# The hybrid layer's third up product at 256 columns, z in groups of 272/384/384 at one distance, weight tiles of one size, and splits on VectorE

## The chip, the core and the metric

The kernel runs on one core of a Trainium2 chip. The time is the device time of one execution in microseconds; the figure that counts is the median over several executions. Before the change it is 1257.54 us (three runs, 1257.53 to 1258.32).

A core has a matrix engine (TensorE, PE in the profile, with its weight loads shown apart as PEld), three engines for elementwise work (VectorE or DVE, ScalarE or ACT, GpSimd or POOL) and an engine that issues most of the DMA transfers (SyncE or SP). The engines run on their own and wait for each other by semaphores. Operands lie in SBUF, 128 partitions wide; matmul results are collected in PSUM.

## What is computed

One layer of a hybrid decoder in float32, on 1024 tokens with 16 meta tokens in front (1040 rows) and width 1024:

```python
h = layer_norm(concat([meta, x]), in_ln_g, in_ln_b)
z = h @ w_in + b_in
q, k, v, c_in, gates = split(z)            # 512, 128, 128, 1024, 2048
a = swa_sink_attention(q, k, v, sinks)     # window 128, 8 heads, 2 kv heads
c = c_val * sigmoid(c_gate)                # halves of c_in
c = silu(layer_norm(causal_dwconv(c, conv_dw, conv_dw_b)))   # 31 taps
mixed = sigmoid(g_attn) * (a @ w_attn_proj) + sigmoid(g_conv) * (c @ w_conv_proj)
h = layer_norm(alpha * h + mixed @ w_out)
up = causal_dwconv(h @ ffn_w_up)           # 2 x 2816 columns, 3 taps
u, g = split(up)
h = layer_norm(alpha * h + (gelu(g) * u) @ ffn_w_down)
return h[:, 16:]
```

## The kernel before

Every matrix product is done in the fp32r type, with both operands split into a high and a low part: for each 128 rows of the contraction there are three matmuls, high by high (L301), high by low (L305) and low by high (L306). The weights are the stationary operand, 128 x 128 at a time, and the activations (transposed, so that tokens run along the free axis) are the moving one.

In order of time the stages are: the opening with the first LayerNorm, the transposes and the first z tiles (0 to 60 us); z tiles with the conv's chunks (60 to 165); attention, with further z tiles as filler between its matmuls (165 to 350); the rest of the gates' z tiles (350 to 416); the two projections and their merging with the gates, by eight output blocks m (416 to 515); the output product with its LayerNorm (515 to 640); the up stage (to 1037); the down stage and the last LayerNorm (to the end).

z: a z tile is 128 columns of w_in, that is, 128 rows of the transposed z, over all tokens. `z_tile` (L316) loads and splits its weights with `weights` (L281) and runs three groups of tokens, 24 matmuls each (8 pieces of the contraction, three matmuls). The groups of the eight conv tiles are ZG: 400, 384 and 256 columns; those of the three q tiles and the sixteen gate tiles are TG, the same without the first 14 tokens: 386, 384 and 256. k, v and the first q tile run in the opening, in the groups HG (272, 384, 384), with matmuls at L514 and L517. The normalized input's high and low parts, the moving operand, lie in the wide tiles RHO (first four pieces of the contraction) and RHC (last four). `h0` (L255) gives their place: piece k, part hl starts at (2k + hl) x 1040 floats, which is 65 times 64 bytes.

Weights: `wraw_p` holds two raw tiles. `wsp_p` holds two pairs of tiles `whi` and `wlo`. A `wlo` tile is 64 columns wider than a `whi` tile; z uses it from column 16 on (`shift=16`), the projections from column 0. The up stage takes the same tiles for the ring of split weights (`wsplit`, L1318), and the last LayerNorm for its rows (`ln_rows`). Counted in units of 64 bytes from the start of a partition, the two `whi` tiles lie at 191 and 255, the two `wlo` tiles at 319 and 387. The raw weights are cast to the high part on ScalarE (L273); the low part is raw minus high (L276), on VectorE for the first 23 tiles that are loaded and on GpSimd for the 15 after them: gates 9 to 15 and the eight blocks of the projections.

Attention's tiles (keys `kx`, values `v`, queries `qt`, scores `s`, probabilities `ph` and `pl`) lie behind the pool `cp` on the right side of SBUF and start 32 bytes off a multiple of 64. Scores are matmuls of 272 columns (L833, L834), sums over values 512 columns (L868 to L870).

The conv on 31 taps runs on VectorE (L669) into four accumulators; `csum` adds them for the conv's LayerNorm, two adds on GpSimd (L886, L887) and one on VectorE (L888).

The up stage uses a Strassen form with seven block products in place of eight, in 22 chunks. A product has two halves of the token columns (`sub` 0 and 1, 258 and 256 columns wide) with 12 matmuls each (L1503). `columns` gives the first column: the first two columns of the first half are left out in two of the seven products, BT3 and B22, which are then 256 wide. `B_AT` says where the right operand of each product lies; that of BT1 in the first half is in the tile RX, at column 16.

The order of work on each engine is set when the program is built, by priorities (`cur_priority`, `rank`) and by extra edges (`after`). `ahead` (L743) is a matmul of gate tile 0, in its second group; the first matmuls of attention are placed behind it.

Of the kernel before, what the change touches and what calls it, by code (L numbers as in the profile page):

```python
# [29 lines left out]
P = 128  # L30
D = 1024
# [17 lines left out]
ALPHA = 2.0 ** 0.25  # L49
NEG = -1e30  # L50


ZG = [(0, 400), (400, 784), (784, 1040)]

HG = [(0, 272), (272, 656), (656, 1040)]
UG = [(0, 258), (258, 642), (642, 1026)]
# [45 lines left out]
def tile_hybrid_layer(  # L102
# [150 lines left out]


    def h0(k, hl, a, b):  # L255
        o = ((k % 4) * 2 + hl) * T
        return (RHO if k < 4 else RHC)[:, o + a:o + b]


    tc.cur_priority = RK_QKV  # L260

    def wsp(name, tag):
        return wsp_p.tile([P, D + (64 if tag == "wlo" else 0)], R, name=name, tag=tag)

    def pair_of(hi, lo, shift=0, shape=None):
        hi, lo = wsp(hi, "whi"), wsp(lo, "wlo")[:, shift:shift + D]
        return [t.rearrange("p (k c) -> p k c", k=KC) for t in (hi, lo)] if shape else [hi, lo]

    def wraw(shape):
        return wraw_p.tile(shape, F, name="wr", tag="wr")  # L270
# [7 lines left out]
    fills = [0]  # L278
    last_fill, last_split = [], []

    def weights(shape, fill, shift=16):  # L281
        fills[0] += 1
        n = fills[0]
        own = n == 3
        raw = sp.tile(shape, F, name="wr3") if own else wraw(shape)
        with rank({1: 13, 2: 18, 3: 17, 4: 23}.get(n, RK_SPLIT)):
            last_fill.append(fill(raw))
        hi, lo = (sp.tile(shape, R, name=t + "3") for t in ("whi", "wlo")) if own else pair_of("whi", "wlo", shift, shape)
        if n <= 3:
            return hi, lo, raw  # L290
        with rank(RK_SPLIT):
            last_split.append(split(raw, hi, lo, n <= 23))
        return hi, lo

    chunks_done = []
# [25 lines left out]
    def in_cols(m):  # L321
        return lambda raw: load(raw, w_z[m])

    TG = [(a + U0 if i == 0 else a, b) for i, (a, b) in enumerate(ZG)]

    st_next = [0]

# [294 lines left out]

    att = ExitStack()
    cp = att.enter_context(tc.tile_pool(name="cin", bufs=2, side="right", reuse_waits="tile"))
    ap = att.enter_context(tc.tile_pool(name="att", bufs=1, side="right", reuse_waits="tile"))

    Kx = [ap.tile([P, NB, 144], R, name=f"kx{g}") for g in range(NKV)]
# [18 lines left out]
    def conv_chunk(c):  # L646
        sig = {}

        def g_evac(g, a, b, ps):
            sig[g] = stage(b - a)  # L650

            nc.scalar.activation(sig[g], ps, AF.Tanh, bias=bcol(10 + c), scale=0.5)
            nc.scalar.activation(sig[g], sig[g], AF.Identity, bias=half_, scale=0.5)

        z_tile(in_cols(10 + c), ZG, g_evac, wt_c1[0] if c == 1 else None)
        cin = cp.tile([P, 16 + T], F, name="cin", tag="cin")
        nc.vector.memset(cin[:, 0:16], 0.0)

        def v_evac2(g, a, b, ps):
            nc.vector.scalar_tensor_tensor(cin[:, 16 + a:16 + b], ps, bcol(6 + c), sig[g], OP.add, OP.mult)  # L660

        z_tile(in_cols(6 + c), ZG, v_evac2, wt_c1[1] if c == 1 else None)
        with rank(RK_CONV + c * 100):
            for j in range(TAPS):
                wc = cdw[:, j * CH + c:j * CH + c + 1]
                if j == 0:
                    nc.vector.tensor_scalar(acc[c], cin[:, j:j + U], wc, cdwb(c), OP.mult, OP.add)
                else:
                    nc.vector.scalar_tensor_tensor(acc[c], cin[:, j:j + U], wc, acc[c], OP.mult, OP.add)  # L669
# [70 lines left out]
    tc.cur_priority = RK_Z - 500  # L740
    first_chunk = len(chunks_done)
    gate_tile(0)
    ahead = chunks_done[first_chunk + KC + 5]  # L743

    tc.cur_priority = RK_ATT

# [130 lines left out]
    for o in order:  # L877
        if isinstance(o, str):
            conv_chunk(int(o[1]))
        else:  # L880
            gate_tile(o)
        if o == "c3":

            csum = cp.tile([P, 16 + T], F, name="csum", tag="cin")[:, :U]
            with rank(RK_EVAC):
                nc.gpsimd.tensor_tensor(csum, acc[0], acc[1], OP.add)  # L886
                nc.gpsimd.tensor_tensor(csum, csum, acc[2], OP.add)  # L887
                nc.vector.tensor_tensor(csum, csum, acc[3], OP.add)  # L888

    def mean_mms(ps, w, hi, lo):  # L890
# [164 lines left out]
    def prep_wo(k, raw=None, behind=None):  # L1055
        if k < 4:
            hi, lo = OA[:, k * 2048:k * 2048 + 1024], OA[:, k * 2048 + 1024:k * 2048 + 2048]
        elif k < 6:
            hi, lo = ((RX, RW)[k - 4][:, x:x + 1024] for x in (0, 1024))
        else:  # L1060
            hi, lo = pair_of("whi", "wlo")
        if raw is None:
            raw = wraw([P, D])
            load(raw, w_out_v[k])
# [17 lines left out]
    tc.cur_priority = RK_PROJ  # L1082
    early = []
    for m in range(KC):
        hi, lo = weights([P, KC, P], lambda raw: load(raw, w_ab[m]), 0)

        def branch(i, g, tag, bufs):
            a, b = PG[g]
# [56 lines left out]
    def quadrant(sub, kk, h):  # L1145
# [1 line left out]
        return FA[:, h1_at(sub, i):h1_at(sub, i + 4)]  # L1147


    B_AT = [[(RHC, 6224), (RHO, 4112), (OA, 16), (RX, 16), (OA, 2096), (OA, 6224), (OA, 4144)],  # L1150
            [(OC, 48), (OC, 2096), (OC, 4144), (OC, 6192), (RHC, 2096), (RHC, 48), (RHC, 4144)]]
    B11, B21, BT2, BT1, BT3, BT4, B22 = range(7)

    def columns(sub, q):

        a, b = SUB[sub]
        return (2 if q in (BT3, B22) else a) if sub == 0 else a, b

    def bsum(sub, q, hl):
        a, b = columns(sub, q)  # L1160
# [152 lines left out]
    def wsplit(src):  # L1313
# [1 line left out]
        ring_next[0] += 1  # L1315
        i %= len(RING)
        if RING[i] is None:
            RING[i] = wsp("ws", ("whi", "wlo")[i % 2])[:, 0:D]  # L1318
        t = RING[i]
        hi, lo = t[:, 0:512], t[:, 512:1024]  # L1320
        nc.scalar.copy(hi, src)  # L1321
# [339 lines left out]
    extra = []  # L1661

    def ln_rows(names):
        return [wsp_p.tile([P, D + (64 if t == "wlo" else 0)], F, name=n, tag=t)[:, 0:D]
                for n, t in zip(names, ("whi", "wlo"))]

    gains = ln_rows(("g1", "b1"))
    g1, b1 = gains
# [127 lines left out]
```

## Time and profile before

| | |
|---|---|
| median of three runs | 1257.54 us |
| profiled execution, its time | 1257.53 us |
| profiled execution, span of the trace | 1255.4 us |
| TensorE busy | 1244.7 us (99% of the span) |
| VectorE busy | 1086.2 us (87%) |
| ScalarE busy | 586.4 us (47%) |
| GpSimd busy | 54.0 us (4%) |
| DMA | 212.10 MB, mean 169 GB/s |

The span is the time from the first to the last record of the trace; the time of the execution has some 2 us around it. A matmul's busy time is longer than its share of the engine, since matmuls overlap in the pipeline: what one costs is the time from its start to the start of the next, and a window that begins at the first matmul of a group and ends at the first of the next holds just that. The chain that ended last is followed back from the last instruction to whatever released it; with 97% on PE, it is a list of matmuls.

### The profile page before, as it was taken

To read this page: it belongs to the slowest core of one execution; us is meant where nothing else is said; L and a number is where in the kernel's file an instruction comes from. 1 tells how busy PE (TensorE), PEld (TensorE's weight loads), DVE (VectorE), ACT (ScalarE), POOL (GpSimd) and SP (SyncE) were. 2 spreads that over 40 slices of the span, in tenths; PEclk is the share of its full clock that TensorE was granted. 3 is DMA by queue.
4 is the path that set the end of the run, shared out by engine and by line. 5 is a ranking of instruction groups with operands and counts; after the bars stand their busy time and mean duration, and the time that the engine had idled before them with its cause. 6 is when DMAs were issued, how large, how long until landed. Compare 5 with 4: busy or idle time off the path is not lost.

```text
span 1255.4 us, 21714 instructions
## 1 busy us (share of the span) xinstructions
PE 1244.7 (99%) x8546; PEld 1178.1 (94%) x8546; DVE 1086.2 (87%) x1859; ACT 586.4 (47%) x1057; POOL 54.0 (4%) x28
## 2 busy tenths in 40 slices
PE   9999999999999999999999999999999999999997
PEld 8999999999999999788899999999999998888886
DVE  7899989999989587548899999999999986995697
ACT  7522244545474223235565555554555554544330
POOL 0000000010112132000000000000000000000000
PEclk9999999999999999999999999999999999999999
DMA  7294733332246565212145555563464569988722
GB/s 279 72 306 108 193 96 97 106 92 84 68 142 177 155 172 140 85 68 101 68 135 192 193 204 192 185 212 115 162 228 166 203 213 319 389 322 300 251 85 84
DMA packets 96152, 212.10 MB, mean 169 GB/s; under 512 B 10787, under 2 KB 35939, under 8 KB 95922
## 3 DMA queue, kind: packets, MB, share of 16 engines
q1 hardware_dynamic: 84282, 199.64, 47.8%
q10 hardware_dynamic: 11768, 11.08, 2.7%
q8 instruction: 67, 1.10, 0.4%
q14 instruction: 35, 0.29, 0.1%
HBM read 150.29 MB, written 62.70 MB: 170 GB/s over the span
## 4 chain that ended last, share of the span: by engine, by line
PE 97%; DVE 1%; ACT 1%; DMA 0%; issue 0%; SPq 0%; DVEq 0%
PE px L1503 15%; PE py L1503 9%; PE ps_x L1641 9%; PE ps_z L305 8%; PE ps_z L301 8%; PE ps_z L306 8%; PE ps_z L1641 7%; PE pz L1503 5%; PE pw L1503 5%; PE ps_p L301 2%; PE ps_p L306 2%; PE ps_p L305 2%; PE ps_w L306 2%; PE ps_w L301 2%; PE ps_w L305 2%; PE ps_z L517 2%
## 5 line engine op out<-in xcount | busy, mean ns | idle before, releaser
L669 DVE SCALAR_TENSOR_TENSOR FA<-cin,cols,FA 128x1026 f32<-128x1026 f32 x120 | 155.2, 1305 | 0.2
L301 PE MATMUL ps_z<-RHO,whi 128*128 128x384 f32 (+2 forms) x324 | 104.6, 323 | 0.0
L305 PE MATMUL ps_z<-RHC,whi 128*128 128x384 f32 (+2 forms) x324 | 104.6, 323 | 0.0
L305 PE MATMUL ps_z<-RHO,whi 128*128 128x384 f32 (+2 forms) x324 | 104.0, 321 | 0.0
L306 PE MATMUL ps_z<-RHC,wlo 128*128 128x384 f32 (+2 forms) x324 | 103.8, 320 | 0.0
L301 PE MATMUL ps_z<-RHC,whi 128*128 128x384 f32 (+2 forms) x324 | 103.7, 320 | 0.0
L306 PE MATMUL ps_z<-RHO,wlo 128*128 128x384 f32 (+2 forms) x324 | 103.4, 319 | 0.0
L1322 DVE TENSOR_TENSOR RHO<-wr,RHO 128x512 fp32r<-128x512 f32 x94 | 63.9, 689 | 5.4 <-ACT RHO L1321 5.4
L1321 ACT CAST RHO<-wr 128x512 fp32r<-128x512 f32 x94 | 56.8, 620 | 23.0 <-DVE wr L1339 12.0
L273 ACT CAST whi<-wr 128x1024 fp32r<-128x1024 f32 x37 | 38.9, 1051 | 53.8 <-PE ps_z L305 32.3
L301 PEld LDWEIGHTS ps_z<-RHO,whi 128*128 128x128 f32 x324 | 60.9, 188 | 0.5 <-issue 0.3
L305 PEld LDWEIGHTS ps_z<-RHC,whi 128*128 128x128 f32 x324 | 60.9, 188 | 0.4
L306 PEld LDWEIGHTS ps_z<-RHC,wlo 128*128 128x128 f32 x324 | 60.9, 188 | 0.2
L301 PEld LDWEIGHTS ps_z<-RHC,whi 128*128 128x128 f32 x324 | 60.9, 188 | 0.2
L306 PEld LDWEIGHTS ps_z<-RHO,wlo 128*128 128x128 f32 x324 | 60.9, 188 | 0.1
L305 PEld LDWEIGHTS ps_z<-RHO,whi 128*128 128x128 f32 x324 | 60.9, 188 | 0.1
L1339 DVE TENSOR_TENSOR wr<-wr 128x512 f32<-128x512 f32 x88 | 60.8, 691 | 0.2
L276 POOL TENSOR_TENSOR wlo<-wr,whi 128x1024 fp32r<-128x1024 f32 x17 | 42.2, 2485 | 183.4 <-ACT whi L273 183.4
L676 ACT ACTIVATE FA<-ps_z,cols 128x386 f32<-128x386 f32 (+2 forms) x48 | 26.0, 541 | 47.1 <-PE ps_z L306 43.1
L1515 ACT COPY FA<-px 128x514 f32<-128x514 f32 (+2 forms) x23 | 13.1, 570 | 70.2 <-PE px L1503 70.2
L1322 DVE TENSOR_TENSOR ws<-wr,ws 128x512 fp32r<-128x512 f32 x60 | 40.9, 690 | 4.7 <-ACT ws L1321 4.6
L1428 ACT ACTIVATE FA<-OB,cols 128x512 f32<-128x512 f32 x44 | 35.9, 816 | 13.7 <-DVE OB L1511 13.7
(467 smaller groups left out, 3568.3 us busy)
## 6 DMA issues: line engine op xcount, KB each, us to landing
wr<-in_w_up_dram SPq DMA_DIRECT2D x44, 512.0 KB, 4.2
wr<-in_w_z_dram SPq DMA_DIRECT2D x30, 512.0 KB, 3.5
fd<-FA SPq DMA_DIRECT2D x44, 256.0 KB, 2.5
OB<-in_w_down_dram SPq DMA_DIRECT2D x19, 512.0 KB, 6.3
qt<-qd SPq DMA_DIRECT2D x28, 256.0 KB, 3.8
td<-OB SPq DMA_DIRECT2D x12, 512.0 KB
sums<-fd SPq DMA_DIRECT2D x12, 512.0 KB, 4.4
sd<-sums SPq DMA_DIRECT2D x12, 512.0 KB, 2.7
```

What stands on the lines that cost most here:

```text
L273: ins = nc.scalar.copy(hi, raw)
L276: return (nc.vector if quick else nc.gpsimd).tensor_tensor(lo, raw, f32(hi), OP.subtract)
L301: ins = nc.tensor.matmul(ps, ah, bh, start=i == 0, stop=False)
L305: nc.tensor.matmul(ps, ah, bl, start=False, stop=False)
L306: last = nc.tensor.matmul(ps, al, bh, start=False, stop=i == n - 1)
L669: nc.vector.scalar_tensor_tensor(acc[c], cin[:, j:j + U], wc, acc[c], OP.mult, OP.add)
L1321: nc.scalar.copy(hi, src)
L1322: ins = nc.vector.tensor_tensor(lo, src, f32(hi), OP.subtract)
L1339: ins = nc.vector.tensor_tensor(*x)
L1428: nc.scalar.activation(t, cc[:, 2:HW], AF.Identity, bias=ffw(3, o), scale=ffw(2, o))
L1503: ins = nc.tensor.matmul(o, x[:, ks], bmat(sub, q, hl, k), start=first and k + j == 0, stop=k == 3 and j == 2, skip_group_check=not first)
L1641: nc.tensor.matmul(banks[i], l[:, ts], r[:, ws], start=first and a and x + k == 0, stop=z and x == len(ops) - 1 and k == 2, skip_group_che ...
```

## The change

- `columns`: BT1 leaves out the first two columns as well, so that five of the seven products have 258 + 256 columns before and four after; its operand in RX moves from column 16 to 48.
- z: ZG goes; conv tiles use HG (272, 384, 384) and TG is made from it (258, 384, 384). `h0` stores the normalized input group by group, so that high and low parts of a group follow one another at 272 or 384 floats (17 or 24 times 64 bytes).
- Weight tiles are all 1024 columns wide, without the shift. The two `wlo` tiles lie at 319 and 383, in units of 64 bytes.
- All weight tiles of z and of the projections are split on VectorE, where the two adds of `csum` are done as well. GpSimd keeps the splits of four blocks of w_out (`prep_wo`, k = 4 to 7).
- A tile of 32 bytes (`pad_i`) in front of attention's tiles moves these to a multiple of 64 bytes.
- `ahead` is taken from gate tile 0's third group (its second piece of the contraction), before from its second group (the sixth piece).

```diff
--- before.py
+++ after.py
@@ -50,8 +50,6 @@
 NEG = -1e30
 
 
-ZG = [(0, 400), (400, 784), (784, 1040)]
-
 HG = [(0, 272), (272, 656), (656, 1040)]
 UG = [(0, 258), (258, 642), (642, 1026)]
 
@@ -253,18 +251,14 @@
 
 
     def h0(k, hl, a, b):
-        o = ((k % 4) * 2 + hl) * T
-        return (RHO if k < 4 else RHC)[:, o + a:o + b]
+        g = next(g for g, x in enumerate(HG) if a < x[1])
+        x, y = HG[g]
+        i, n = (k % 4) * 2 + hl, y - x
+        o = i * n + ((6144 if i else 0), 272, 3344)[g]
+        return (RHO if k < 4 else RHC)[:, o + a - x:o + b - x]
 
 
     tc.cur_priority = RK_QKV
-
-    def wsp(name, tag):
-        return wsp_p.tile([P, D + (64 if tag == "wlo" else 0)], R, name=name, tag=tag)
-
-    def pair_of(hi, lo, shift=0, shape=None):
-        hi, lo = wsp(hi, "whi"), wsp(lo, "wlo")[:, shift:shift + D]
-        return [t.rearrange("p (k c) -> p k c", k=KC) for t in (hi, lo)] if shape else [hi, lo]
 
     def wraw(shape):
         return wraw_p.tile(shape, F, name="wr", tag="wr")
@@ -278,18 +272,19 @@
     fills = [0]
     last_fill, last_split = [], []
 
-    def weights(shape, fill, shift=16):
+    def weights(shape, fill):
         fills[0] += 1
         n = fills[0]
         own = n == 3
         raw = sp.tile(shape, F, name="wr3") if own else wraw(shape)
         with rank({1: 13, 2: 18, 3: 17, 4: 23}.get(n, RK_SPLIT)):
             last_fill.append(fill(raw))
-        hi, lo = (sp.tile(shape, R, name=t + "3") for t in ("whi", "wlo")) if own else pair_of("whi", "wlo", shift, shape)
+        hi, lo = (sp.tile(shape, R, name=t + "3") if own else wsp_p.tile(shape, R, name=t, tag=t)
+                  for t in ("whi", "wlo"))
         if n <= 3:
             return hi, lo, raw
         with rank(RK_SPLIT):
-            last_split.append(split(raw, hi, lo, n <= 23))
+            last_split.append(split(raw, hi, lo, True))
         return hi, lo
 
     chunks_done = []
@@ -321,7 +316,7 @@
     def in_cols(m):
         return lambda raw: load(raw, w_z[m])
 
-    TG = [(a + U0 if i == 0 else a, b) for i, (a, b) in enumerate(ZG)]
+    TG = [(a + U0 if i == 0 else a, b) for i, (a, b) in enumerate(HG)]
 
     st_next = [0]
 
@@ -622,6 +617,7 @@
 
     att = ExitStack()
     cp = att.enter_context(tc.tile_pool(name="cin", bufs=2, side="right", reuse_waits="tile"))
+    cp.tile([P, 8], F, name="pad_i", tag="pad", bufs=1)
     ap = att.enter_context(tc.tile_pool(name="att", bufs=1, side="right", reuse_waits="tile"))
 
     Kx = [ap.tile([P, NB, 144], R, name=f"kx{g}") for g in range(NKV)]
@@ -652,14 +648,14 @@
             nc.scalar.activation(sig[g], ps, AF.Tanh, bias=bcol(10 + c), scale=0.5)
             nc.scalar.activation(sig[g], sig[g], AF.Identity, bias=half_, scale=0.5)
 
-        z_tile(in_cols(10 + c), ZG, g_evac, wt_c1[0] if c == 1 else None)
+        z_tile(in_cols(10 + c), HG, g_evac, wt_c1[0] if c == 1 else None)
         cin = cp.tile([P, 16 + T], F, name="cin", tag="cin")
         nc.vector.memset(cin[:, 0:16], 0.0)
 
         def v_evac2(g, a, b, ps):
             nc.vector.scalar_tensor_tensor(cin[:, 16 + a:16 + b], ps, bcol(6 + c), sig[g], OP.add, OP.mult)
 
-        z_tile(in_cols(6 + c), ZG, v_evac2, wt_c1[1] if c == 1 else None)
+        z_tile(in_cols(6 + c), HG, v_evac2, wt_c1[1] if c == 1 else None)
         with rank(RK_CONV + c * 100):
             for j in range(TAPS):
                 wc = cdw[:, j * CH + c:j * CH + c + 1]
@@ -740,7 +736,7 @@
     tc.cur_priority = RK_Z - 500
     first_chunk = len(chunks_done)
     gate_tile(0)
-    ahead = chunks_done[first_chunk + KC + 5]
+    ahead = chunks_done[first_chunk + 2 * KC + 1]
 
     tc.cur_priority = RK_ATT
 
@@ -883,8 +879,8 @@
 
             csum = cp.tile([P, 16 + T], F, name="csum", tag="cin")[:, :U]
             with rank(RK_EVAC):
-                nc.gpsimd.tensor_tensor(csum, acc[0], acc[1], OP.add)
-                nc.gpsimd.tensor_tensor(csum, csum, acc[2], OP.add)
+                nc.vector.tensor_tensor(csum, acc[0], acc[1], OP.add)
+                nc.vector.tensor_tensor(csum, csum, acc[2], OP.add)
                 nc.vector.tensor_tensor(csum, csum, acc[3], OP.add)
 
     def mean_mms(ps, w, hi, lo):
@@ -1058,7 +1054,7 @@
         elif k < 6:
             hi, lo = ((RX, RW)[k - 4][:, x:x + 1024] for x in (0, 1024))
         else:
-            hi, lo = pair_of("whi", "wlo")
+            hi, lo = (wsp_p.tile([P, D], R, name=n, tag=n) for n in ("whi", "wlo"))
         if raw is None:
             raw = wraw([P, D])
             load(raw, w_out_v[k])
@@ -1082,7 +1078,7 @@
     tc.cur_priority = RK_PROJ
     early = []
     for m in range(KC):
-        hi, lo = weights([P, KC, P], lambda raw: load(raw, w_ab[m]), 0)
+        hi, lo = weights([P, KC, P], lambda raw: load(raw, w_ab[m]))
 
         def branch(i, g, tag, bufs):
             a, b = PG[g]
@@ -1147,14 +1143,14 @@
         return FA[:, h1_at(sub, i):h1_at(sub, i + 4)]
 
 
-    B_AT = [[(RHC, 6224), (RHO, 4112), (OA, 16), (RX, 16), (OA, 2096), (OA, 6224), (OA, 4144)],
+    B_AT = [[(RHC, 6224), (RHO, 4112), (OA, 16), (RX, 48), (OA, 2096), (OA, 6224), (OA, 4144)],
             [(OC, 48), (OC, 2096), (OC, 4144), (OC, 6192), (RHC, 2096), (RHC, 48), (RHC, 4144)]]
     B11, B21, BT2, BT1, BT3, BT4, B22 = range(7)
 
     def columns(sub, q):
 
         a, b = SUB[sub]
-        return (2 if q in (BT3, B22) else a) if sub == 0 else a, b
+        return (2 if q in (BT1, BT3, B22) else a) if sub == 0 else a, b
 
     def bsum(sub, q, hl):
         a, b = columns(sub, q)
@@ -1315,7 +1311,7 @@
         ring_next[0] += 1
         i %= len(RING)
         if RING[i] is None:
-            RING[i] = wsp("ws", ("whi", "wlo")[i % 2])[:, 0:D]
+            RING[i] = wsp_p.tile([P, D], R, name="ws", tag=("whi", "wlo")[i % 2])
         t = RING[i]
         hi, lo = t[:, 0:512], t[:, 512:1024]
         nc.scalar.copy(hi, src)
@@ -1661,8 +1657,7 @@
     extra = []
 
     def ln_rows(names):
-        return [wsp_p.tile([P, D + (64 if t == "wlo" else 0)], F, name=n, tag=t)[:, 0:D]
-                for n, t in zip(names, ("whi", "wlo"))]
+        return [wsp_p.tile([P, D], F, name=n, tag=t) for n, t in zip(names, ("whi", "wlo"))]
 
     gains = ln_rows(("g1", "b1"))
     g1, b1 = gains
```

## The prediction

> **What bounds the kernel now.** I read the page's busy times and slices first, then the chain that ended last, then PE's waits.
>
> ```profile
> span 1255.4 us, 21714 instructions
> PE 1244.7 (99%) x8546; PEld 1178.1 (94%) x8546; DVE 1086.2 (87%) x1859; ACT 586.4 (47%) x1057; POOL 54.0 (4%) x28
> PEclk9999999999999999999999999999999999999999
> PE 97%; DVE 1%; ACT 1%; DMA 0%; issue 0%; SPq 0%; DVEq 0%
> ```
>
> ```profile
> PE ps_w L541 <- DVE ones_r L222: 1.1, 1, 1.1
> PE pw L1503 <- ACT FA L1304: 1.0, 1, 1.0
> ```
>
> TensorE is the bound from end to end, at full clock, and it hardly waits. So the change can win only by making a matmul take less time from its start to the next one's start, and it can lose by making one take more, or by making TensorE wait for VectorE, which is the next engine. The windows by stage show where VectorE is full (columns after the window: its length, then busy time and instruction count of PE, PEld, DVE, ACT, POOL, then clock, DMA share, GB/s):
>
> ```profile
> 225.00:285.00 60.00, 60.00 (x401) 58.45 (x399) 58.02 (x117) 31.43 (x81) 4.00 (x2) 1.00 0.35 96
> 285.00:350.00 65.00, 65.00 (x423) 62.91 (x422) 61.93 (x114) 33.95 (x86) 7.15 (x3) 1.00 0.23 76
> 350.00:416.00 66.00, 66.00 (x423) 65.79 (x422) 58.68 (x112) 36.48 (x57) 13.53 (x6) 1.00 0.63 167
> ```
>
> **The change part by part.** Up stage: BT1 is the product that reads RX. Its matmuls of the first half of the columns are 258 wide, 156 and 108 by the tile that holds the weights, together 264 = 22 chunks x 12.
>
> ```profile
> L1503 PE MATMUL py<-RX,RHO 128*128 128x258 f32 x156 | 20.7, 281 | 0.0
> L1503 PE MATMUL py<-RX,ws 128*128 128x258 f32 x108 | 14.4, 282 | 0.0
> ```
>
> The chain between 640 and 670 us gives the products of a chunk (start, us, what); BT1 is the one at 641.62, and the two behind it are BT3 and B22, which have 256 columns already:
>
> ```profile
> 641.62 2.79 PE py L1503 x24
> 644.41 2.72 PE px L1503 x24
> 647.13 2.72 PE py L1503 x24
> ```
>
> BT1 goes from 2.79 to 2.72: 0.07 x 22 = **-1.5 us**. TensorE runs without a gap there, so nothing hides it. The same matmul 256 wide costs 2.72 / 24 = 113.3 ns; I use it as the price of a clean matmul. (The Trainium skill, "TensorE: Matmul & The Clock Gate", section on the back-to-back issue gap, gives N/2.4 + 2.5 ns; by it two columns less are 0.8 ns each, 0.2 us in all. The rows show 0.07 / 12 = 5.8 ns, so they decide.)
>
> Groups of z: three windows hold one whole group of 24 matmuls each of a gate tile, two more the first two groups of a conv tile:
>
> ```profile
> 386.62:390.83 4.21, 4.21 (x25) 4.21 (x25) 4.11 (x6) 0.58 (x1) 2.10 (x1) 1.00 0.56 150
> 390.83:393.66 2.83, 2.83 (x26) 2.83 (x25) 2.62 (x8) 0.58 (x1) 0.00 (x0) 1.00 0.84 224
> 393.66:397.93 4.27, 4.27 (x26) 4.27 (x25) 4.17 (x6) 1.42 (x2) 2.60 (x1) 1.00 0.84 177
> 79.36:83.71 4.35, 4.35 (x27) 4.35 (x25) 3.91 (x11) 1.05 (x1) 0.00 (x0) 1.00 1.02 412
> 83.71:87.93 4.22, 4.22 (x26) 4.22 (x26) 4.00 (x9) 1.22 (x2) 0.00 (x0) 1.00 1.03 406
> ```
>
> The 256 group takes 2.83 where the same matmuls take 2.72 in the up stage; by 256 : 384 a clean 384 group would be 4.08 and it takes 4.21. So z pays 0.11 to 0.13 us a group, about 5 ns a matmul, and the up stage does not. What differs in the program: in the up stage hi and lo of the moving operand lie 64 or 32 pieces of 64 bytes apart, in z 65, so that the position modulo 512 bytes changes with every operand. After the change the two 384 groups have a distance of 24 pieces, a multiple of 8, as in the up stage; the 258/272 group has 17. I therefore price a 384 group at 4.08 to 4.09 (between 4.08 and today's 4.21), and the short group by the 258-wide matmuls of the projections, two groups of 12:
>
> ```profile
> 438.72:441.62 2.90, 2.90 (x26) 2.90 (x25) 2.09 (x4) 1.41 (x2) 1.65 (x1) 1.00 0.66 109
> ```
>
> 2.90, and up to 3.01 where it keeps 0.11. A q or gate tile goes from 4.21 + 2.83 + 4.27 = 11.31 to 2.90 + 2 x 4.08 = 11.06: -0.25, x 19 tiles = -4.8. A conv tile goes from 4.35 + 4.22 + 2.83 = 11.40 to 3.00 + 8.17 = 11.17: -0.23, x 8 = -1.8. Not all of it is collected: 12 of the 27 tiles are fillers between attention's matmuls, where about 6 in 10 z matmuls follow one another directly. 15 x 0.24 + 12 x 0.24 x 0.6 = 5.3, of which I take nine tenths, **-4.8 us** (ends: 0, and -6.6). The first z, 144 more matmuls at 384 columns (L517), could give 144 x 5 ns = 0.7; it is fed piece by piece by the opening, so **-0.3** (0 to -0.7).
>
> Attention's tiles move by 32 bytes. Its scores are 272 wide, 17 pieces like the 258 above (2.90 / 24 = 120.8 ns); its sums over values are 512 wide like the output product's:
>
> ```profile
> 263.04 0.29 PE L833 MATMUL ps_s<-kx,qt 128*128 128x272 f32 x1
> 263.29 0.34 PE L301 MATMUL ps_z<-RHC,whi 128*128 128x384 f32 x1
> 266.89 0.39 PE L868 MATMUL ps_o<-ph,v 128*128 128x512 f32 x1
> 267.82 0.39 PE L870 MATMUL ps_o<-pmT,vm 128*128 128x512 f32 x1
> 511.09 0.39 PE L306 MATMUL ps_w<-RX,RHC 128*128 128x512 f32 x1
> 512.00 0.39 PE L301 MATMUL ps_w<-OA,RHC 128*128 128x512 f32 x1
> ```
>
> Two scores take 0.25 (L833 and L834 up to the next), 125 ns each; four value matmuls 0.93, 232 ns each, against 0.91 / 4 = 228 ns in the output product. So 112 x 4 ns + 76 x 5 ns = **-0.8 us** (0 to -1.3).
>
> Weight tiles: the lo half of every second pair moves from piece 387 (388 in z) to 383, so that hi and lo of both pairs now stand at 7 modulo 8. The projections have both kinds side by side: in odd m both halves are at 7, in even m hi is at 7 and lo at 3. Five whole groups of 12 matmuls each, first an odd m, then an even one:
>
> ```profile
> 430.24:437.31 7.07, 7.07 (x63) 7.07 (x62) 5.09 (x12) 1.23 (x4) 0.76 (x1) 1.00 0.50 132
> 441.62:448.43 6.81, 6.81 (x62) 6.81 (x61) 5.08 (x12) 1.17 (x4) 0.75 (x1) 1.00 0.76 242
> ```
>
> 7.07 against 6.81, 4.3 ns a matmul. After the change even m has the odd one's addresses: six groups x 0.052 = 0.31 a tile, x 4 = **+1.2 us**. Against it speaks the up stage, where the two halves of a weight lie 32 pieces apart in one tile, so at one position modulo 512 bytes as well, and 256-wide matmuls take the clean 113.3; so the bounds are 0 and +1.2, and I take the upper one, for the same loop and operands. (The Trainium skill, same page, section on the steps of a matmul: TensorE has two independent read ports, and loading weights doesn't steal bandwidth from the running matmul. By it no address of a weight tile could change the time. 7.07 beside 6.81 differ in nothing else that the program shows, so the trace does not agree.)
>
> GpSimd's work moves to VectorE: 15 splits and two adds of csum.
>
> ```profile
> L276 DVE TENSOR_TENSOR wlo<-wr,whi x20: 1160/1217/1224, 52.3 to 304.1; 128x1024 fp32r<-128x1024 f32 x20
> 375.79 2.40 POOL L276 TENSOR_TENSOR wlo<-wr,whi 128x1024 fp32r<-128x1024 f32 x1 [12.32 <-ACT whi L273]
> 375.82 2.52 DVE L984 CAST OC<-FA 128x258 fp32r<-128x258 f32 x1
> 378.73 0.29 DVE L984 CAST OC<-FA 128x258 fp32r<-128x258 f32 x1
> 279.01 2.00 POOL L886 TENSOR_TENSOR csum<-FA 128x1026 f32<-128x1026 f32 x1 [275.70 <-DVE FA L669]
> ```
>
> A split is 1.22 on VectorE, 2.40 on GpSimd; but VectorE's cast that began beside it took 2.52 instead of 0.29, so GpSimd's split costs VectorE 2.2 already. Moved, VectorE gains up to 1.0 a split in the gates' stage, and loses 1.2 where nothing collided. csum adds 2 x 1.2 near 280 us. On VectorE a split waits for ScalarE's cast of the high part (the releaser in the POOL row, whi L273), and behind it in the queue stand attention's scores, conv's splits (L984 to L997) and, later, the merges of the projections; TensorE's transposes (ps_t) wait for the first of these, the projections for the second. The work that hides all this is TensorE's own queue. It is thinnest where the projections begin: the last split of conv's output ends at 413.1, the first matmul that follows the gates is at 416.27:
>
> ```profile
> 412.58 0.56 DVE L997 TENSOR_TENSOR OA<-OB,OA 128x384 fp32r<-128x384 f32 x1
> 416.27 0.28 PE L301 MATMUL ps_p<-OA,whi 128*128 128x258 f32 x1
> ```
>
> That is 3.1 us, while z comes up to 5 us earlier and the five collisions after 350 us give VectorE up to 5 back. I take **0**; without that cover it would be +2. Both engines hold no DMA issue of these tiles in the way: loads go out from SP in the same order and number. `ahead` lets attention's fillers start 0.6 us of work later: 0.
>
> Sum: -1.5 - 4.8 - 0.3 - 0.8 + 1.2 = **-6.2 us**. The profiled execution took 1257.53 (span 1255.4 + 2.1 around it), the median of the three runs is 1257.54: **1251.3 us**.
>
> **The rivals.**
> (1) z's gain is half lost: around 290 to 330 us TensorE is tied to VectorE's pace (61.93 busy of 65 above), where the filler tiles' gain would turn into waiting, and the conv tiles' with it. z gives -2.4: 1253.7.
> (2) The layout gives nothing in z. For it: the 386 group starts off a 64-byte boundary and takes 4.27, just 25/24 of a clean 4.08 (4.25), with the same 65-piece distance, so distance is not all; and the odd m's show the same 4 to 5 ns at constant positions. Then -1.5 - 0.8 + 1.2 = -1.1: 1256.4, no change. (By the Trainium skill's rule on ports above, only BT1 is left: by the row 1256.0, in this case as well.)
> (3) Slower: both halves of the weights at one position modulo 512 bytes is the costly case itself, as in the odd m's, and it now holds for every z tile on top of what z pays: 27 x 72 matmuls x 4.3 ns = 8.4, with +1.2 in the projections, -1.5 and -0.8: +7.3, 1264.8. It decides from a 384 group above 4.21 on. Against it: today's z has lo at 0 or 4 modulo 8 beside hi at 7 and pays anyway, so its price may be the same one already; and the up stage has equal positions too and pays nothing.
>
> **How the numbers follow.** Forecast 0.63 (its own range 1248.5 to 1253), rival 1 0.14, rival 2 0.13, rival 3 with a late start of the projections 0.10. Likeliest: 1251.3. Lower end: all of z, first z and attention, no cost in the projections, -1.5 - 6.6 - 0.7 - 1.3 = -10.1, 1247.4; upper end 1256.6 takes rival 2 in and leaves rival 3 out. A measurement tells 0.2%, 2.5 us, from no change: faster (under 1255.0) 0.77, same 0.13, slower 0.10.
>
> **What would show it.** Right: 384 groups of z at 4.08 to 4.12 in undisturbed gate tiles, the short one at 2.87 to 3.0; three products of 2.72 in a chunk; the even m's at 7.07 for five groups; scores at 121 ns; no new wait of PE on DVE. Wrong: 384 groups at 4.21 (rival 2) or above (rival 3), or PE gaps before ps_t or ps_p that DVE releases.

## The result and the profile after

The changed kernel takes 1255.63 us (median of 19 runs, 1255.00 to 1256.37) where the kernel before takes 1257.90 in the same series (19 runs, 1257.41 to 1258.32). The ratio is 0.9982, 95% interval 0.9975 to 0.9989: a gain of 2.3 us. The forecast was 6.2. The time lies in the stated range, but only a third of the likeliest case's gain is there. The profiled execution took 1255.65, with a span of 1253.9 where the one before has 1255.4. Some 0.35 us of the gain lies outside the span, where no matmul stands: the time around it is 2.07 to 2.20 us in every execution of the kernel before and 1.75 to 1.85 with the change. It goes with the splits: 2.07 to 2.18 us in the two runs below that put them back on GpSimd with all else changed. The prediction took this time as fixed, and what it holds was not traced.

The page's busy times and the chain after the change:

```profile
PE 1241.6 (99%) x8546; PEld 1174.7 (94%) x8546; DVE 1081.1 (86%) x1876; ACT 586.7 (47%) x1056; POOL 12.3 (1%) x11
PE 95%; DVE 3%; DMA 1%; issue 1%; ACT 0%; SPq 0%; DVEq 0%
```

TensorE is still the bound. VectorE is busy 5 us less although it has 17 instructions more. The chain now has a piece that is not TensorE's, and PE's waits say where:

```profile
PE ps_w L536 <- DVE ones_r L220: 1.1, 1, 1.1
PE pw L1499 <- ACT FA L1300: 1.0, 1, 1.0
PE ps_h L462 <- DVE xn L426: 1.0, 1, 1.0
PE ps_s L829 <- DMA qt<-qd: 0.9, 1, 0.9
```

The wait for xn, at 9 us, was 0.2 before and differs from one execution to the next (up to 1.6 in the profiles below); it takes nothing from the first z matmul, which starts at 56.49 us against 56.46. The wait for `qt` is new.

Where the time came from, by the start of the same matmul in the two traces:

| matmul | before | after | difference |
|---|---|---|---|
| first of z after the opening | 56.46 | 56.49 | 0.0 |
| first of the last gate tile | 404.96 | 404.82 | -0.1 |
| first of the projections | 416.27 | 416.04 | -0.2 |
| first of the output product (L296, before L301) | 503.03 | 503.12 | +0.1 |
| first of the down stage (L1637, before L1641) | 1037.83 | 1036.28 | -1.6 |

So nearly all of what the two traces differ by came in the up stage, and z, where the forecast had most, gave 0.2. Now the windows of a gate tile, group by group, and of five groups of 12 in the projections, first an even m, then an odd one:

```profile
382.38:385.28 2.90, 2.90 (x26) 2.90 (x25) 1.78 (x5) 2.86 (x4) 0.00 (x0) 1.00 0.00 0
385.28:389.44 4.16, 4.16 (x26) 4.16 (x25) 2.05 (x3) 3.00 (x5) 0.00 (x0) 1.00 0.15 51
389.44:393.60 4.16, 4.16 (x25) 4.16 (x25) 4.02 (x10) 2.93 (x5) 0.00 (x0) 1.00 0.64 158
420.35:427.41 7.06, 7.06 (x62) 7.06 (x61) 4.07 (x11) 1.06 (x3) 0.00 (x0) 1.00 0.36 143
431.69:438.49 6.80, 6.80 (x63) 6.80 (x61) 4.03 (x11) 1.10 (x3) 0.00 (x0) 1.00 0.44 119
```

The short group takes the 2.90 of the forecast, the 384 groups 4.16 and not 4.08. A gate tile is 11.22 against 11.31: -0.09, not -0.25. The even m pays now and the odd one is free; before it was the other way round. The chain of the up stage shows three products of 2.72 in a chunk:

```profile
641.62 2.72 PE py L1499 x24
644.34 2.72 PE px L1499 x24
647.06 2.72 PE py L1499 x24
649.78 2.79 PE px L1499 x24
```

All up matmuls together, from each start to the next, take 426.33 us against 428.00: -1.7.

### The profile page after: what moved, and what is told of

It is laid out like the page before. It is cut to its first block, busy times and chain, and to the rows that moved or that the text cites. A ratio compares the mean times of both kernels' runs of the same rounds, so it can differ in the third digit from the quotient of the medians.

```text
span 1253.9 us, 21702 instructions
## 1 busy us (share of the span) xinstructions
PE 1241.6 (99%) x8546; PEld 1174.7 (94%) x8546; DVE 1081.1 (86%) x1876; ACT 586.7 (47%) x1056; POOL 12.3 (1%) x11
## 4 chain that ended last, share of the span: by engine, by line
PE 95%; DVE 3%; DMA 1%; issue 1%; ACT 0%; SPq 0%; DVEq 0%
PE px L1499 15%; PE py L1499 10%; PE ps_x L1637 9%; PE ps_z L1637 7%; PE ps_z L300 7%; PE ps_z L301 7%; PE ps_z L296 7%; PE pw L1499 5%; PE pz L1499 5%; PE ps_p L301 2%; PE ps_p L296 2%; PE ps_p L300 2%; PE ps_w L301 2%; PE ps_w L296 2%; PE ps_w L300 2%; PE ps_z L512 2%
## 5 line engine op out<-in xcount | busy, mean ns | idle before, releaser
L665 DVE SCALAR_TENSOR_TENSOR FA<-cin,cols,FA 128x1026 f32<-128x1026 f32 x120 | 152.5, 1280 | 0.3
L296 PE MATMUL ps_z<-RHO,whi 128*128 128x384 f32 (+2 forms) x324 | 104.2, 322 | 0.0
L301 PE MATMUL ps_z<-RHC,wlo 128*128 128x384 f32 (+2 forms) x324 | 103.8, 320 | 0.0
L296 PE MATMUL ps_z<-RHC,whi 128*128 128x384 f32 (+2 forms) x324 | 103.7, 320 | 0.0
L301 PE MATMUL ps_z<-RHO,wlo 128*128 128x384 f32 (+2 forms) x324 | 103.7, 320 | 0.0
L296 PEld LDWEIGHTS ps_z<-RHO,whi 128*128 128x128 f32 x324 | 61.0, 188 | 0.6 <-issue 0.3
L296 PEld LDWEIGHTS ps_z<-RHC,whi 128*128 128x128 f32 x324 | 61.1, 188 | 0.2
L301 PEld LDWEIGHTS ps_z<-RHO,wlo 128*128 128x128 f32 x324 | 61.0, 188 | 0.2
L301 PEld LDWEIGHTS ps_z<-RHC,wlo 128*128 128x128 f32 x324 | 60.9, 188 | 0.2
L672 ACT ACTIVATE FA<-ps_z,cols 128x384 f32<-128x384 f32 (+1 forms) x48 | 26.1, 543 | 50.3 <-PE ps_z L301 49.3
L270 DVE TENSOR_TENSOR wlo<-wr,whi 128x1024 fp32r<-128x1024 f32 x35 | 42.6, 1218 | 4.8 <-ACT whi L267 4.1
```

What stands on the lines that cost most here:

```text
L270: return (nc.vector if quick else nc.gpsimd).tensor_tensor(lo, raw, f32(hi), OP.subtract)
L296: ins = nc.tensor.matmul(ps, ah, bh, start=i == 0, stop=False)
L301: last = nc.tensor.matmul(ps, al, bh, start=False, stop=i == n - 1)
```

## The experiments

Below, a "step" is the time from a matmul's start to the next one's, and a "clean" step is 170.0 ns for 384 columns and 113.3 for 256, as in the prediction.

**z's groups at other addresses (one execution).** A table in `z_group` gives single groups another start, distance, width or weight tile.

```diff
+    PROBES = {1: probe(17, 32, 64, 384), 2: probe(17, 0, 0, 384), ...
+              64: probe(18, 24, 48, 384), 65: probe(19, 24, 48, 384), ...
+              76: probe(17, 32, 64, 512), 77: probe(19, 32, 64, 512),
+              79: probe(17, 32, 64, 256), 80: probe(19, 32, 64, 256)}
...
+            o = (r0 + (k % 4) * ks + hl * d) * 16 + sub
+            return (RHO if k < 4 else RHC)[:, o:o + n]
```

> Groups of z read the normalized input at other places, so that these groups' sums are not z: in the last six gate tiles 384 columns at one position modulo 512 bytes, 1 to 7 in units of 64 bytes, one start 56 bytes off, then 512 columns at 0 and 2, then 256 at 0 and 2 (twice each); in three conv tiles 384 columns with high to low 32, 0, 28, 25 and 64 units apart, and once the high weights in place of the low. After the change a 384 group of 24 matmuls takes 4.16 us, 3.3 ns a matmul over a clean 170.0. Theory 'relation': the 3.3 ns come from the moving operand standing at 0 beside weights at 7; then at least one other position gives 4.08 (most likely 2 and 6, where the up stage is clean), and distances of 32 and 64 give 4.16 as now. Theory 'width': 384 columns pay 3.3 ns wherever they stand, 4.16 for all seven positions and for all distances that keep one position, and 256 at 2.72 and 512 at 5.44 are clean at 0 and 2 alike. Theory 'rhythm': the extra is a rhythm that TensorE falls into by what runs ahead; all positions give 4.16, and 256 gives 2.72 or 2.83 by its predecessor and not by its position.

The windows that hold one whole undisturbed group, in this order: 384 columns at position 1, 5 and 7 and at a start 56 bytes behind position 0, 512 at 0 and at 2, 256 at 0 and at 2:

```profile
348.73:352.95 4.22, 4.22 (x27) 4.22 (x25) 2.16 (x3) 1.53 (x2) 0.00 (x0) 1.00 0.91 218
...
373.98:378.20 4.22, 4.22 (x26) 4.22 (x25) 2.83 (x6) 4.17 (x6) 0.00 (x0) 1.00 0.62 173
...
385.61:389.77 4.16, 4.16 (x26) 4.16 (x25) 2.07 (x4) 2.94 (x5) 0.00 (x0) 1.00 0.15 51
389.77:394.09 4.32, 4.32 (x25) 4.32 (x25) 4.22 (x10) 2.98 (x5) 0.00 (x0) 1.00 0.59 152
396.99:402.49 5.50, 5.50 (x27) 4.51 (x25) 5.33 (x13) 0.48 (x1) 0.00 (x0) 1.00 0.81 220
402.49:408.08 5.59, 5.59 (x26) 4.51 (x25) 5.32 (x13) 0.62 (x2) 0.00 (x0) 1.00 0.84 222
410.98:413.81 2.83, 2.83 (x26) 2.83 (x25) 2.73 (x6) 0.48 (x1) 0.00 (x0) 1.00 0.86 235
416.64:419.36 2.72, 2.72 (x26) 2.72 (x25) 0.87 (x2) 0.58 (x1) 0.00 (x0) 1.00 0.46 103
```

No 384 group came under 4.16. At positions 3, 4 and 6 conv's matmuls stand between those of the group; the undisturbed steps there exceed 170.0 by some 3.5 ns, as at 0 and 7, and at 1, 2 and 5 they exceed it by 5.7 to 6.5. Distances of 0, 28, 32 and 64 units and the high weights in both places gave 3.3 as well. With a distance of 28 the high part stands at position 0 and the low one at 4, so the change of position cost nothing there; a distance of 25 leads through all eight positions, 1, 2 and 5 among them, and gave 5.5. The start 56 bytes off gave 4.32, 180 ns a matmul; such a start was the 386 group's in the kernel before, which took 4.27. So 384 columns have a floor of 173.3 ns that no address tried removes ("width"), and above it a second part that goes with addresses; each position is one group, so the 5.7 to 6.5 rest on three. "Relation", in which a right position is clean, falls. That 256 is clean at 2 and pays at 0 looks like position; the runs with 256 groups below take that back.

**z's layout and groups undone.** ZG, the old `h0` and the old `ahead` come back, all else stays.

```diff
+ZG = [(0, 400), (400, 784), (784, 1040)]
...
+        o = ((k % 4) * 2 + hl) * T
+        return (RHO if k < 4 else RHC)[:, o + a:o + b]
```

> z's layout and groups as before (400 or 386, 384, 256 at 65 units), all else as after the change. If the new layout is worth what the trace shows (z's matmuls 308.95 us before, 308.61 after with a wait of 0.9 among them), this is 0.3 to 1.2 slower than the changed kernel, 1255.9 to 1256.8, without the wait for the queries. If the layout is worth the forecast 4.8 and something else gave it back: 1258 or more. If it costs: under 1255.3.

1255.74 us (1255.43 to 1256.04), ratio to the kernel before 0.9984 (0.9975 to 0.9993): the same as the changed kernel, and between two of the expected bands. The new layout and groups are worth nothing net. But PE doesn't wait for `qt` here: beside the run with late scores below (1254.97), where it doesn't wait either, they are worth 0.8, which the wait takes back.

**The splits undone.** The 15 splits and two adds of csum run on GpSimd again.

```diff
-            last_split.append(split(raw, hi, lo, True))
+            last_split.append(split(raw, hi, lo, n <= 23))
...
-                nc.vector.tensor_tensor(csum, acc[0], acc[1], OP.add)
-                nc.vector.tensor_tensor(csum, csum, acc[2], OP.add)
+                nc.gpsimd.tensor_tensor(csum, acc[0], acc[1], OP.add)
+                nc.gpsimd.tensor_tensor(csum, csum, acc[2], OP.add)
```

> The 15 splits and the two adds of csum on GpSimd again, all else as after the change. Theory of the prediction: hidden, the same time within 0.4 us, 1255.2 to 1256.0. Rival: VectorE's 15 splits delay attention (the last value matmul is 3.0 us later after the change), then this is faster, 1254 or less. Other rival: GpSimd's collisions with VectorE did delay TensorE, then 1256.5 or more.

1260.13 us (1259.23 to 1261.11), ratio 1.0018 (1.0009 to 1.0027): 4.5 slower than the changed kernel and slower than the kernel before. The profile's PE waits have two new entries:

```profile
PE ps_z L296 <- ACT FA L672: 1.8, 1, 1.8
PE ps_o L864 <- DVE OB L791: 1.4, 1, 1.4
```

The timeline of the second of these (start, length, engine, what):

```profile
333.35 2.40 POOL L270 TENSOR_TENSOR wlo<-wr,whi 128x1024 fp32r<-128x1024 f32 x1 [10.52 <-ACT whi L267]
333.59 3.25 DVE L665 SCALAR_TENSOR_TENSOR FA<-cin,cols,FA 128x1026 f32<-128x1026 f32 x1
336.87 0.69 DVE L791 TENSOR_TENSOR OB<-OB,ps_o 64x512 f32<-64x512 f32 x1
337.61 0.50 PE L864 MATMUL ps_o<-ph,v 128*128 128x512 f32 x1 [1.36 <-DVE OB L791]
```

A conv step that takes 1.27 takes 3.25 beside GpSimd's split, the add that frees attention's PSUM stands behind it, and TensorE waits. In the kernel before, the stretched conv step stood behind that add and hit nobody:

```profile
334.41 2.40 POOL L276 TENSOR_TENSOR wlo<-wr,whi 128x1024 fp32r<-128x1024 f32 x1 [14.19 <-ACT whi L273]
334.63 0.69 DVE L795 TENSOR_TENSOR OB<-OB,ps_o 64x512 f32<-64x512 f32 x1
335.36 2.54 DVE L669 SCALAR_TENSOR_TENSOR FA<-cin,cols,FA 128x1026 f32<-128x1026 f32 x1
```

(The Trainium skill, "SBUF — State Buffer", section "Who interferes with whom", has GpSimd and VectorE share one pair of ports as an exclusive lock, and a VectorE instruction with two SBUF inputs contend for it with a GpSimd one that reads SBUF. The 3.25 beside 1.27 agrees.)

The first of the two waits is another matter. ScalarE's evacuation that ends it stands in ScalarE's queue behind a cast, a table load and an activation, with no idle time among them:

```profile
377.84 1.04 ACT L267 CAST whi<-wr 128x1024 fp32r<-128x1024 f32 x1
378.91 1.28 ACT L974 ACT_TABLE_LOAD   x1
380.20 0.71 ACT L974 ACTIVATE FA<-FA,cols 128x384 f32<-128x384 f32 x1
380.81 0.56 ACT L672 ACTIVATE FA<-ps_z,cols 128x384 f32<-128x384 f32 x1
381.43 0.44 PE L296 MATMUL ps_z<-RHO,whi 128*128 128x384 f32 x1 [1.84 <-ACT FA L672]
```

VectorE did have an instruction stretched to 2.39 just then, but it ended at 381.86, when the evacuation was over. So this wait comes from the order on ScalarE, which the edit changed as well; the runs don't show how much of that order is due to the collisions. With the old groups the place of the splits matters little: 1256.31 with the splits on GpSimd (BT1 alone, below) and 1255.74 in the run above with them on VectorE, with new weight tiles and the pad in it.

**The first scores later.** The first score matmul is held back by four triples of z.

```diff
+                if i == g == r == 0:
+                    after(ins, chunks_done[first_chunk + KC + 6])
```

> The first matmul of attention's scores is placed four triples later in gate tile 0, all else as after the change. After the change TensorE waits 0.9 us at 141.7 us for the queries' DMA, with z matmuls queued behind. If that wait is lost time: 0.7 to 0.9 faster, 1254.7 to 1254.9. If attention sets the end of its stage and the wait is made up later by fillers: the same, 1255.4 to 1255.9.

1254.97 us (1254.60 to 1255.90), ratio 0.9979 (0.997 to 0.9988). The wait for `qt` is gone from PE's waits, and the time is 0.7 under the changed kernel's median, as the lost-time reading has it. All runs below keep this edit, except the last one, BT1 alone.

**The splits undone with the scores late.** The edits of the last two together, to see whether the 4.5 us was an accident of one order.

> GpSimd's splits and csum adds as before the change, now with the scores late; all else as after the change. With the splits on VectorE this is 1254.97. In the run with GpSimd's splits alone undone TensorE waited twice, 1.4 and 1.8 us, each time behind a VectorE instruction that a GpSimd split had stretched by 2 us. Theory 'lock': with the new groups these collisions always cost TensorE, 1258 to 1259.5. Theory 'accident of order': which instruction is hit depends on the order, so with the scores at another place it is another cost, likely smaller: 1255.3 to 1257.

1259.28 us (1258.51 to 1260.70), 4.3 above 1254.97. The order differs and the two waits are the same ones, 1.8 for the gates' evacuation and 1.3 for L791. The time is that of "lock", but its reason holds for L791 alone, since here too the evacuation runs straight behind a table load and an activation. The two profiled spans differ by 3.3 us (1256.9 and 1253.6), of which the two waits are 3.1; 0.3 lies outside the span, and the rest of the 4.3 is the difference of these executions from their medians.

**z in four groups, three of 256.** The 384 groups become 256 groups, the normalized input behind the first group is stored 768 columns a piece; two runs, at position 2 and at position 0. The scores are late here too, held by another matmul of gate tile 0.

```diff
+ZG = [(0, 272), (272, 528), (528, 784), (784, 1040)]
...
+        i = (k % 4) * 2 + hl
+        o = i * 272 + (6144 if i >= 3 else 0) if a < 272 else 544 + i * 768
+        return (RHO if k < 4 else RHC)[:, o + a:o + b]
```

> z in four groups, 258 or 272 and three times 256, with the normalized input behind the first group stored 768 columns a piece, at position 2 modulo 512 bytes (units of 64 bytes); the scores late as in the run before. Theory 'width' (a 384 group can't take less than 4.16, a 256 group can take 2.72): a gate tile is 2.90 + 3 x 2.72 = 11.06 against 11.22 after the change, 0.16 x 27 = 4.3 less where nothing disturbs, about 1251.5 to 1253 against 1254.97. Theory 'rhythm' (256 pays 4.4 ns or nothing by what runs ahead): 2.90 + 3 x 2.83 = 11.39, 1257 to 1259.5. One more evacuation a tile on ScalarE is hidden if nothing waits for it.

> The same with the three 256 groups at position 0, where the probe's 256 groups took 2.83 (at 2 they took 2.72). Theory 'position': 11.39 a tile, 5 to 8 us slower than the kernel with position 2. Theory 'rhythm': the same time as that kernel within 0.5 us, since what runs ahead is the same.

1261.91 us (ratio 1.003, 1.0019 to 1.0042) and 1264.62 (1.0048, 1.0035 to 1.0062). At position 2 two groups of different tiles, same addresses modulo 512 bytes:

```profile
108.26:110.99 2.73, 2.73 (x26) 2.73 (x25) 2.73 (x3) 0.89 (x2) 0.00 (x0) 1.00 0.22 56
119.30:122.13 2.83, 2.83 (x27) 2.83 (x25) 2.83 (x4) 0.89 (x2) 0.00 (x0) 1.00 0.52 85
```

A 256 group is clean or pays 4.4 ns at one and the same position, and most pay: of 40 undisturbed groups 12 are clean at position 2 and 4 at position 0. So the position doesn't decide it alone, as "rhythm" has it, but the two runs differ by 2.7 us and not by less than 0.5, so it seems to bear on how often a group pays: without waits z's steps sum to 311.3 and 314.4 us, which is nearly all of the 3.2 between the two spans. The rest of the loss is new: PE waits 1.7 us for VectorE's evacuation of conv's z, 1.5 for ScalarE's of a gate and 0.5 for the queries at position 2. Behind ScalarE's wait the granted clock falls to half:

```profile
379.00:382.60 3.60, 1.83 (x12) 1.53 (x12) 2.39 (x4) 3.14 (x7) 0.00 (x0) 1.00 0.14 41
382.63:386.05 3.42, 3.42 (x18) 3.42 (x17) 3.28 (x8) 3.00 (x4) 0.00 (x0) 0.50 0.75 223
```

A 256-column step takes 212 ns in this stretch instead of some 115. By an estimate from these steps that is 16 x 0.1 = 1.6 us lost. The run at position 0 has the same (0.50 from 384.83 to 388.24); the 1.8 us wait in the run with the splits undone was not followed by it.

**The projections' groups in another order.** Each of the runs moves the 258-wide group of some m to the end.

```diff
-            for g in range(4):
+            for g in (0, 1, 2, 3) if m % 2 else (1, 2, 3, 0):
```

> In the projections the 258-wide group is done last in even m and first in odd m, so that two of them stand together; the scores late as before. After the change m = 0, 2, 4, 6 pay 4.4 ns a matmul in their 256-wide groups and m = 1, 3, 5, 7 pay nothing; before the change it was 1, 3, 5 that paid, at other weight addresses. Theory 'address' (the pair of weight tiles decides): the alternation stays, the projections' matmuls take 89.9 us as now, the time is 1254.97 as in the run with late scores. Theory 'rhythm' (24 matmuls of 258 columns turn the paying state into the free one and back): 48 of them turn it twice, so it stays what it is at the start, and the projections take 88.7 (all free, 1253.8) or 91.2 (all paying, 1256.2).

1256.27 us, ratio 0.9986 (0.9977 to 0.9995). Five groups from the end of m = 1 into m = 2 take what an odd m took before the change, and so do all others:

```profile
431.94:439.01 7.07, 7.07 (x63) 7.07 (x61) 4.31 (x11) 2.17 (x4) 0.00 (x0) 1.00 0.41 94
```

The projections' steps sum to 91.03 us, as "rhythm" had it. The second order leaves one single block of 258 between m = 0 and m = 1:

```diff
-            for g in range(4):
+            for g in (1, 2, 3, 0) if m % 2 or m == 0 else (0, 1, 2, 3):
```

> The 258-wide group last in m = 0, 1, 3, 5 and first in 2, 4, 6, so that one block of 24 such matmuls stands alone between m = 0 and m = 1 and all later ones stand in pairs; the scores late as before. Theory 'rhythm': m = 0 pays as in the run with all pairs, the single block turns the state, the pairs keep it: m = 1 to 6 are free, the projections' matmuls take about 88.8 us instead of 89.9 (alternating) or 91.0 (all paying), and the time is 1253.9 beside 1254.97 and 1256.27. Theory 'address': 89.9 and 1255.0.

```profile
428.13:434.93 6.80, 6.80 (x63) 6.80 (x61) 4.87 (x12) 1.09 (x3) 0.00 (x0) 1.00 0.42 117
440.71:447.53 6.82, 6.82 (x63) 6.82 (x61) 4.34 (x12) 1.18 (x4) 0.00 (x0) 1.00 0.71 228
```

m = 0 pays, m = 1 to 6 are free, the sum is 88.92, and the time 1254.12 us (1253.76 to 1254.49), ratio 0.9972 (0.9961 to 0.9983): the fastest kernel of this study, 1.5 under the changed kernel's median.

**The weight tiles undone.** Low tiles 64 columns wider and z from column 16 on, as before the change; scores late.

```diff
+        return wsp_p.tile([P, D + (64 if tag == "wlo" else 0)], R, name=name, tag=tag)
...
+        hi, lo = wsp(hi, "whi"), wsp(lo, "wlo")[:, shift:shift + D]
```

> Weight tiles as before the change (low tiles 64 columns wider, z from column 16 on, low halves at 319 and 387), the scores late, all else as after the change. Theory 'address' of the prediction: z's 384 groups or the projections change by an amount that goes with the tile pair. Theory 'rhythm': 384 groups stay at 4.16 to 4.17, the projections alternate as always (89.6 or 89.9), the time is 1254.97 within 0.5 us.

1256.75 us (1256.55 to 1257.42), 1.8 above 1254.97. Two 384 groups of a gate tile:

```profile
385.85:390.06 4.21, 4.21 (x26) 4.21 (x25) 2.12 (x4) 2.94 (x5) 0.00 (x0) 1.00 0.14 51
390.06:394.27 4.21, 4.21 (x25) 4.21 (x25) 4.11 (x10) 2.98 (x5) 0.00 (x0) 1.00 0.61 156
```

This is a miss of the expectation from "rhythm": with the new layout, the groups go from 4.16 to 4.21 when only the weights' addresses change; all 25 undisturbed groups take 4.21, and the 384 steps sum to 229.79 us against 227.61. The projections alternate as ever (89.91 in both). So with this layout the weight tiles at one position are worth 1.8 us, in z alone. Neither half is worth anything without the other: z's steps sum to 308.94 us in the kernel before, 309.12 with the new weight tiles and the old layout, 309.58 here and 307.67 with both and the scores late. One thing does not fit an account by addresses alone: in the kernel before, with its old addresses, 2 of 12 undisturbed 384 groups took 4.16 as well (those at 96.09 and 375.37 us), so a rhythm may play a part in z, too. (The Trainium skill's rule that loading weights doesn't steal from the running matmul, from "TensorE: Matmul & The Clock Gate", section on the steps of a matmul, read as the prediction reads it, would make the two kernels equal in z; 4.21 beside 4.16 does not agree.)

**Attention's tiles 32 bytes off again**, scores late (`pad_i` left out).

> Attention's tiles 32 bytes off a multiple of 64 as before the change, the scores late, all else as after the change. The prediction's term of 0.8 us: 1255.7. What the trace after the change shows (the median step from one score matmul to the next stays at 125 ns and that of a value matmul at 232): no difference, 1254.97 within 0.4 us.

1254.49 us (1254.21 to 1255.45), 0.5 below 1254.97, with overlapping spreads. The alignment is worth nothing: the median step of the first score matmul of a pair is 125 ns and that of a value matmul 232, with the pad 125 and 232.

**BT1 alone**, on the kernel before.

```diff
-        return (2 if q in (BT3, B22) else a) if sub == 0 else a, b
+        return (2 if q in (BT1, BT3, B22) else a) if sub == 0 else a, b
```

> The kernel before with BT1 at 256 columns and its operand at column 48, nothing else of the change. The up stage's matmuls take 426.33 us after the change against 428.00, so this gives -1.7: 1256.1 (1255.8 to 1256.4). If all else of the change together is worth nothing, this equals the changed kernel, 1255.6; if the change's other parts cost time, it is below that.

1256.31 us (1255.81 to 1256.98), ratio 0.9987 (0.9978 to 0.9995): -1.5. All else of the change together gives 0.7 more.

## Why the prediction was right or wrong

- **BT1, -1.5: right.** -1.5 by the run with this edit alone.
- **z's groups, -4.8: the step that failed.** The prediction took a clean 384 group for one and a half clean 256 groups, 4.08, and named a changing position as what keeps z from it. The probe shows that 384 columns have a floor of 4.16 at every position and distance tried, so 0.08 of the 0.13 that it took for a 384 group was never to be had. The rest of the way, from 4.21 to 4.16, is real. The run with the old weight tiles shows that the new layout gets it only with the weight tiles at one position; by the probe the moving operand must keep off the positions 1, 2 and 5, while a change between 0 and 4 costs nothing, so that the changing position as such was not the cause. Per gate tile that left 0.09 of 0.25. All z steps sum to 308.61 us against 308.94, with the new 0.9 us wait among them; with the scores late, without that wait, it is 307.67. So the term measured -1.3, and -0.3 with the wait.
- **The first z, -0.3: nothing.** The steps of L517 (L512 after the change) sum to 25.92 us against 25.80.
- **Attention, -0.8: nothing.** 125 and 232 ns a step before, after, and with the pad taken out. The difference from the clean step comes from something else than the 32 bytes.
- **Projections, +1.2: mis-read.** Odd and even m did differ by 0.26 in five groups, but not by weight tile: 24 matmuls of 258 columns turn a paying state into a free one and back, and the state in which m = 0 begins is set ahead of it (with the old groups and the new weight tiles the projections took 89.59 as before the change). After the change the two kinds changed places, 89.91 against 89.59: +0.3. So these rows were no evidence against the rule on the two read ports (the Trainium skill, "TensorE: Matmul & The Clock Gate", section on the steps of a matmul), as the prediction had them: in the projections the weights' addresses made no difference (89.91 with the old ones and with the scores late). It is z, with 4.21 beside 4.16, that doesn't agree with it.
- **Splits and csum on VectorE, 0: right as a sum, wrong in weight.** The cover did hold, and no wait for them arose. But with GpSimd the changed kernel takes 4.3 to 4.5 more: 1.3 to 1.4 because attention's add now stands behind an instruction that a collision stretches, 1.8 by an evacuation that stands late in ScalarE's queue, 0.3 outside the span. The prediction counted only what the splits cost VectorE and not what queued behind the collision, nor that moving them changes the order on ScalarE.
- **`ahead`, 0: wrong by 0.7.** TensorE came to the first score matmul at 140.8 us and waited until 141.7 for the queries' DMA, with z's matmuls queued behind; before the change it started there at 142.0 without a wait. The edit to `ahead` does not hold these matmuls; the run with late scores gave 0.7 back.
- **The rivals.** The second, layout worth nothing and 1256.4, is the one that came nearest in time and for z's total. Its time is partly luck, since it had -0.8 for attention and +1.2 for the projections, where the runs show 0 and +0.3. That z pays at constant positions too was right, but the odd m's, which it gave as evidence, pay by the alternating state and not by the floor; its other reason, that the 386 group's start off a 64-byte boundary costs, fits the probe's 4.32.

The balance by the runs: BT1 -1.5; the layout with the splits still on GpSimd +3.8 (1260.13 less 1256.31, with tiles and pad in it); the splits on VectorE -4.5 (1255.63 less 1260.13). That makes -2.2; it must come near the 2.3 measured, since each difference starts where the last one ends, and it doesn't show that the parts would have these sizes in another order.

## What to carry to other kernels

A price scaled from one width to another is not a row: no whole group of 384 columns was ever seen at 4.08, and one probe with several widths and addresses in one kernel would have said so. Where two halves of a loop alternate between two prices, look at the state that one leaves for the next before blaming what differs in their operands; an order with the odd block in pairs tests it. And an engine that stretches another's instructions costs by what stands behind the stretched one, so an edit that only reorders work can make it pay. A wait that appears beside such collisions still has to be followed back by itself: one of the two here came from another queue.

## What the runs showed of the hardware that was not expected

A 384-column matmul took at least 173.3 ns from start to start beside 113.3 for 256 (clean) and about 226.7 for 512 in the down stage; none of eight positions and six distances went below it, and positions 1, 2 and 5 took 175.7 to 176.5. 256-column matmuls of the same loop at the same addresses run at 113.3 or at 117.8 for whole groups, and stay so until matmuls of another width stand between; 24 of 258 columns turned the state every time in the projections, 48 left it as it was; the 12 at the start of m = 7 turned a paying state (after the change) and left a free one (before it). What the state is was not found. With the new layout the weights' position in SBUF changed a 384-column step from 173.3 to 175.4 ns (groups of 4.16 and 4.21 us) with nothing else changed. A start 32 bytes off a multiple of 64 changed nothing for attention's 272 and 512 columns, while one group of 384 columns at a start 56 bytes off took 180 ns a matmul beside 173.3. The granted clock fell to 0.50 for 3.42 us after a stretch of 3.60 us in which TensorE was busy for 1.83.
